# A fifth PSUM bank per pair, and one of two down tiles issued inside it

## The chip, the cores and the metric

The kernel runs on one core of a Trainium2 chip. The metric is the device time of one execution in microseconds (us); smaller is better. The core's engines are called here as the profile calls them: PE is the matmul engine TensorE and PEld its weight loads, DVE is VectorE, ACT is ScalarE, POOL is GpSimd, and SP is the engine whose queue issues nearly all loads. PSUM is the memory that matmuls write, in eight banks; only DVE and ACT read it here.

## The reference: what is computed

Two layers of a hybrid decoder, for a prompt of 512 tokens and 8 x 4 sample tokens, 544 columns in all. Model width is 1024, FFN width 2752, embedding width 256. One layer is

```
h += 0.5 * SwiGLU_a(RMSNorm(h))           # FFN, weights w1_a, w3_a, w2_a
u  = RMSNorm(h); proj = u @ w_in          # state-space heads and window attention
h += concat(ssd_out, attn_out) @ w_out
h += 0.5 * SwiGLU_b(RMSNorm(h))           # FFN, weights w1_b, w3_b, w2_b
h += sigmoid(RMSNorm(h) @ w_ple_gate) * (p[i] @ w_ple_proj)   # embedding
SwiGLU(x) = (silu(x @ w1) * (x @ w3)) @ w2
```

The outputs are h and the states and caches of both layers. There are four FFNs in the whole, and the change touches these and the last line, the embedding step.

## The kernel before

**Layout.** h is held transposed in SBUF: 8 chunks of 128 rows by 544 columns, the columns in two halves of 272. Every product is made of fp32 split into a high and a low part, three matmuls for one: weight-high x x-high, weight-high x x-low, weight-low x x-high. ACT casts the high part of a weight (L100), DVE subtracts for the low part (L101). In the profile the weights of plain products are named wh and wl, those of sums of weights qh and ql; the operands are XH and XL (norm output), T (sums of blocks of it), U (the FFN's inner activation), EH and EL (the embedding).

**FFN.** `ffn` makes 21.5 column tiles of width 128. The first tile and the rest are done plainly (`plain`). The other 20 are done by `pair`, one tile of w1 and the same tile of w3 together: a scheme of seven block products instead of eight, each 12 matmuls of 272 columns (L354). In the code's order they are f11, g2, g3, g1, f12, f22 and g4. They go to four banks: f11 and then f12 accumulate in pa, g2 in pb, g3 and then f22 in pc, g1 and then g4 in pd. Between the two uses of a bank its first content is read: ACT copies pa to v[0] (L362), DVE subtracts pb (L364), makes v[1] = v[0] - pc (L366) and c2's second half = v[1] + pd (L368). Then come c2's first half and t (L370, L372, L374), POOL's multiplication by the norm (L375), tanh on ACT (L248), DVE (L249), POOL (L250), the product c2 (L377), and the split of the result into U, high part on ACT (L259) and low part on DVE (L260). The weights' sums are made by POOL (L338, L339) and DVE (L340, L345).

**Down projection.** Every four pairs fill one U. While the next four pairs run, the eight output tiles of the U before are made, two per pair: `down` is a `gemm` of 2 x 24 / 2 matmuls, 24 per tile, into two banks (L126), and DVE adds the banks to h (L325). For the first four pairs of an FFN it is `plain_down`, of 10 matmuls per tile, with the U of `plain`. After the last pair, eight `down` tiles of the last U remain.

**Embedding.** `ple_prep` loads the embedding rows (L1115, L1116; the tile pt takes memory that the FFN held), transposes them on PE (L1122, L1124), and splits them into EH and EL (ACT L1125, L1126; DVE L1127, L1128). `ple` then runs, for each of eight output tiles, the gate product (48 matmuls with XH and XL) and the projection (12 with EH and EL). In the first tile the norm's sums (L169) and its spreading (L181) stand between them.

**What sets the order.** Each engine runs its instructions in order. That order is made when the program is built: a list scheduler takes instructions in the code's order as their priority and moves a later one ahead where it reckons an earlier one not to be ready. So the code's order is a wish, and the built order tells what runs. Banks come from one pool of eight (`bank()`).

Of the kernel before, what the change touches and what calls it, by code (L numbers as in the profile page):

```python
# [16 lines left out]
DEPTH = 2  # L17
# [6 lines left out]
HN = N // 2  # L24
# [15 lines left out]
def hymba_step(ctx: ExitStack, tc: tile.TileContext, I, O):  # L40
# [9 lines left out]
    def bank():  # L50
        return psp.tile([128, 512], F32, tag="ps", name="ps")
# [84 lines left out]
    HALF = (slice(0, HN), slice(HN, N))  # L136
# [97 lines left out]
    def ffn(g, w1, w3, w2, begun=None):  # L234
# [5 lines left out]
        with tc.tile_pool(name="ffn", bufs=2, reuse_waits="tile") as fp:  # L240
# [17 lines left out]
            def keep(U, i, u):  # L258
                A.copy(U[:, 0, i, :], u)  # L259
                V.tensor_sub(U[:, 1, i, :], u, U[:, 0, i, :].bitcast(F32))  # L260
# [64 lines left out]
                    V.scalar_tensor_tensor(h[:, m, HALF[a]], ps[a][:, 0:HN], f, h[:, m, HALF[a]], op0=ALU.mult, op1=ALU.add)  # L325


            def pair(j, sums, U, i):
                def unit(w, k, pool, tag, bufs):
                    src = w[k * 512:(k + 1) * 512, j * 128:(j + 1) * 128].rearrange("(k p) m -> p k m", p=128)  # L330
                    return raw_unit([(lambda t: t, src)], pool, tag, bufs)

                a11 = unit(w1, 0, fp, "ra", 4)
                a21, a22 = unit(w3, 0, wp, "raw", None), unit(w3, 1, wp, "raw", None)
                a12 = unit(w1, 1, fp, "ra", 4)
                f11 = split(a11)
                q1 = fp.tile([128, KU, 128], F32, tag="q1", name="q1")
                G.tensor_tensor(q1, a21, a22, op=ALU.add)  # L338
                G.tensor_tensor(a21, a21, a11, op=ALU.add)  # L339
                V.tensor_tensor(a11, a11, q1, op=ALU.add)  # L340
                g2 = split(a11, KU, fp, "q", 4)
                g3 = split(a21, KU, fp, "q", 4)
                g1 = split(q1, KU, fp, "q", 4)
                f12 = split(a12)
                V.tensor_tensor(a12, a12, a11, op=ALU.add)  # L345
                f22 = split(a22)
                g4 = split(a12, KU, fp, "q", 4)
                t2, t3, t1, t4 = sums
                x11, x21, x22 = ((XH[:, k:k + KU, c:c + HN], XL[:, k:k + KU, c:c + HN]) for k, c in ((0, 0), (KU, 0), (KU, HN)))

                def prod(ps, f, x, start):
                    for k in range(KU):
                        for n, (lhsT, rhs) in enumerate(terms3([f], k, x[0][:, k, :], x[1][:, k, :])):
                            PE.matmul(ps[:, 0:HN], lhsT, rhs, start=start and k == 0 and n == 0, stop=k == KU - 1 and n == 2,  # L354
                                      skip_group_check=not start)

                pa, pb, pc, pd = bank(), bank(), bank(), bank()
                v = fp.tile([128, 2, HN], F32, tag="v", name="v")
                t = fp.tile([128, N], F32, tag="t1", name="t")
                c2 = fp.tile([128, N], F32, tag="c2", name="c2")  # L360
                prod(pa, f11, x11, True)
                A.copy(v[:, 0, :], pa[:, 0:HN])  # L362
                prod(pb, g2, t2, True)
                V.tensor_sub(v[:, 0, :], v[:, 0, :], pb[:, 0:HN])  # L364
                prod(pc, g3, t3, True)
                V.tensor_sub(v[:, 1, :], v[:, 0, :], pc[:, 0:HN])  # L366
                prod(pd, g1, t1, True)
                V.tensor_tensor(c2[:, HALF[1]], v[:, 1, :], pd[:, 0:HN], op=ALU.add)  # L368
                prod(pa, f12, x21, False)
                V.tensor_tensor(t[:, HALF[0]], pa[:, 0:HN], Rb[:, HALF[0]], op=ALU.mult)  # L370
                prod(pc, f22, t4, False)
                V.tensor_sub(c2[:, HALF[0]], v[:, 0, :], pc[:, 0:HN])  # L372
                prod(pd, g4, x22, False)
                V.tensor_tensor(t[:, HALF[1]], v[:, 0, :], pd[:, 0:HN], op=ALU.add)  # L374
                G.tensor_tensor(t[:, HALF[1]], t[:, HALF[1]], Rb[:, HALF[1]], op=ALU.mult)  # L375
                th = gated(t)
                V.tensor_tensor(c2, c2, th, op=ALU.mult)  # L377
                keep(U, i, c2)

            def down(j0, U, m):  # L380
                src = w2[j0 * 128:(j0 + PH) * 128, m * 128:(m + 1) * 128].rearrange("(k p) m -> p k m", p=128)
# [5 lines left out]
            for j0 in range(1, NJ, PH):  # L387
                U = uset()
                for i in range(PH):
                    pair(j0 + i, sums, U, i)  # L390
                    for m in range(2 * i, 2 * i + 2):
                        last(m)
                last = lambda m, U=U, j0=j0: down(j0, U, m)
            for m in range(KD):
                last(m)
# [732 lines left out]
            V.tensor_tensor(EL[:, c, NP:N], p1[:, 0:NS], EH[:, c, NP:N].bitcast(F32), op=ALU.subtract)  # L1128
        return EH, EL

    def ple(l, P, lp, E, last):
        EH, EL = E
        wg, wpj = I["w_ple_gate"][l], I["w_ple_proj"][l]
        first = piece(wg, 0, 0, KD)
        norm = Norm(P["gp"])
# [14 lines left out]
        for m in range(KD):  # L1150
            pg = xgemm(first if m == 0 else piece(wg, 0, m * 128, KD))
            if m == 0:
                norm.sums()
            p = piece(wpj, 0, m * 128, 2)
            pe = gemm([[t for k in range(2) for t in terms3(p, k, EH[:, k, :], EL[:, k, :])]])
            if m == 0:
# [43 lines left out]
    for l in range(DEPTH):  # L1200
# [7 lines left out]
        mix(l, P)  # L1208
        ffn(P["g2"], I["w1_b"][l], I["w3_b"][l], I["w2_b"][l])
        with tc.tile_pool(name="ple", bufs=2, reuse_waits="tile") as lp:  # L1210
            E = ple_prep(l, lp)
            Pn = params(l + 1) if l + 1 < DEPTH else None
            ple(l, P, lp, E, l == DEPTH - 1)
        P = Pn


# [62 lines left out]
```

## Time and profile before

| | |
|---|---|
| median of 3 runs | 2238.54 us (2235.72 to 2247.51) |
| profiled execution | 2239.0 us, its span 2237.2 us |
| PE busy | 2132.8 us (95%), mean granted clock 0.979 |
| DVE, ACT, POOL busy | 1814.2 (81%), 963.4 (43%), 693.4 (31%) us |
| HBM read, written | 187.56 MB, 9.53 MB |
| L354, matmuls of `pair` | 6720 |

PE is the engine that is busy nearly always, so time is to be had where it stands still or where its granted clock is low. Idle time of another engine costs nothing by itself. An average over the span hides that the stages differ; the prediction reads single stages. A row of the timeline or of a group names line, engine, operation, out<-in, shapes and count; a bracket at its end gives the idle time of the engine before it and what ended it.

### The profile page before, as it was taken

The page shows a single profiled execution, that of the slowest core. Times are in us where ns is not written, and L with a number is a line of the kernel's source. Part 1 is how long each engine was busy: PE and PEld are TensorE (multiplying, and loading weights), DVE is VectorE, ACT ScalarE, POOL GpSimd, SP SyncE. Part 2 cuts the span into 40 slices and gives each one's busy share as a digit, 9 for nine tenths or more (in the row PEclk, how much of TensorE's full clock was granted, in tenths as well). Part 3 has the DMA queues.
Part 4 walks back from the last instruction along what each step waited for, and adds up shares of the span by engine and source line. Part 5 has one row for each costly group of instructions (what it writes and reads, how often), then busy time and mean ns, then how long its engine had stood idle before and what let it go on. Part 6 is the DMA issues. An engine that isn't in the chain of part 4 may idle for free.

```text
span 2237.2 us, 43389 instructions
## 1 busy us (share of the span) xinstructions
PE 2132.8 (95%) x16706; PEld 2085.6 (93%) x16706; DVE 1814.2 (81%) x3282; ACT 963.4 (43%) x1784; POOL 693.4 (31%) x601
## 2 busy tenths in 40 slices
PE   7889999999999899999988999999999998999999
PEld 6889999998899899999988999999888988999998
DVE  7898987589868899886487889975997798998854
ACT  6344443444345344444363444443443543444443
POOL 5232331233523332322132333222334333322220
PEclk9899999999999999999999999999998999999999
DMA  5343332313242333322223333333232423333222
GB/s 142 95 119 96 90 105 73 82 50 86 58 133 59 104 90 99 96 83 84 76 67 104 91 104 90 93 78 76 58 82 67 115 75 105 91 101 97 77 70 76
DMA packets 401211, 197.89 MB, mean 88 GB/s; under 512 B 40270, under 2 KB 400358, under 8 KB 401004
## 3 DMA queue, kind: packets, MB, share of 16 engines
q1 hardware_dynamic: 399420, 194.93, 31.9%
q8 instruction: 132, 2.16, 0.4%
q14 instruction: 75, 0.61, 0.1%
q10 hardware_dynamic: 1584, 0.18, 0.0%
HBM read 187.56 MB, written 9.53 MB: 88 GB/s over the span
## 4 chain that ended last, share of the span: by engine, by line
PE 68%; DVE 19%; issue 4%; POOL 4%; DMA 3%; ACT 1%; POOLq 0%; SPq 0%; DVEq 0%; ACTq 0%
PE ps L126 34%; PE ps L354 29%; DVE wl L101 4%; DVE CV L654 2%; DVE ql L101 2%; POOL th L250 1%; DMA raw<-in_w_a 1%; PE ps L900 1%; DMA raw<-in_w_b 1%; DVE wk L517 1%; DVE XL L155 1%; DVE c L377 1%; DVE ra L345 1%; POOL q L338 1%; DVE th L249 1%
## 5 line engine op out<-in xcount | busy, mean ns | idle before, releaser
L126 PE MATMUL ps<-U,wh 128*128 128x272 f32 x2752 | 526.4, 289 | 0.0
L100 ACT CAST wh<-raw 128x512 fp32r<-128x512 f32 (+1 forms) x448 | 264.8, 596 | 439.6 <-PE ps L126 241.1
L126 PEld LDWEIGHTS ps<-U,wh 128*128 128x128 f32 x2752 | 434.9, 189 | 0.0
L126 PE MATMUL ps<-U,wl 128*128 128x272 f32 x1408 | 402.3, 288 | 0.0
L101 DVE TENSOR_TENSOR wl<-raw,wh 128x512 fp32r<-128x512 f32 (+1 forms) x448 | 313.1, 702 | 72.6 <-ACT wh L100 64.9
L126 PE MATMUL ps<-XH,wh 128*128 128x272 f32 x1184 | 352.2, 300 | 8.9 <-DVE wk L517 4.3
L126 PE MATMUL ps<-XL,wh 128*128 128x272 f32 x1184 | 345.6, 293 | 4.1 <-DVE XL L155 4.0
L126 PE MATMUL ps<-XH,wl 128*128 128x272 f32 x1152 | 336.6, 293 | 0.0
L126 PEld LDWEIGHTS ps<-U,wl 128*128 128x128 f32 x1408 | 266.1, 189 | 0.0
L354 PE MATMUL ps<-T,qh 128*128 128x272 f32 x1280 | 246.7, 289 | 0.8 <-ACT qh L100 0.8
L126 PEld LDWEIGHTS ps<-XH,wh 128*128 128x128 f32 x1184 | 227.5, 193 | 14.6 <-DVE wk L517 4.7
L126 PEld LDWEIGHTS ps<-XL,wh 128*128 128x128 f32 x1184 | 228.7, 193 | 6.2 <-DVE XL L155 5.6
L338 POOL TENSOR_TENSOR q<-raw 128x512 f32<-128x512 f32 x80 | 115.3, 1442 | 353.8 <-DMA raw<-in_w_b 173.5
L126 PEld LDWEIGHTS ps<-XH,wl 128*128 128x128 f32 x1152 | 222.1, 193 | 0.0
L375 POOL TENSOR_TENSOR t<-t,Rb 128x272 f32<-128x272 f32 x80 | 68.1, 851 | 465.3 <-DVE t L374 413.4
L354 PEld LDWEIGHTS ps<-T,qh 128*128 128x128 f32 x1280 | 202.3, 189 | 1.2 <-ACT qh L100 1.2
L354 PE MATMUL ps<-XH,wh 128*128 128x272 f32 x640 | 186.0, 291 | 10.4 <-ACT v L362 7.7
L354 PE MATMUL ps<-XH,qh 128*128 128x272 f32 x640 | 187.6, 293 | 7.8 <-DVE c L368 7.8
L354 PE MATMUL ps<-T,ql 128*128 128x272 f32 x640 | 186.3, 292 | 7.5 <-DVE ql L101 7.5
L354 PE MATMUL ps<-XH,ql 128*128 128x272 f32 x640 | 188.2, 294 | 4.1 <-DVE ql L101 4.1
L101 DVE TENSOR_TENSOR ql<-ra,qh 128x512 fp32r<-128x512 f32 x160 | 183.4, 1146 | 7.7 <-ACT qh L100 0.4
L354 PE MATMUL ps<-XL,qh 128*128 128x272 f32 x640 | 188.3, 294 | 0.0
(389 smaller groups left out, 5072.8 us busy)
## 6 DMA issues: line engine op xcount, KB each, us to landing
raw<-in_w_a SPq DMA_DIRECT2D x168, 256.0 KB
raw<-in_w_b SPq DMA_DIRECT2D x168, 256.0 KB
ra<-in_w_a SPq DMA_DIRECT2D x80, 256.0 KB
ra<-in_w_b SPq DMA_DIRECT2D x80, 256.0 KB
raw<-in_w_in SPq DMA_DIRECT2D x60, 256.0 KB
raw<-in_w_ple_gate SPq DMA_DIRECT2D x32, 256.0 KB
raw<-in_w_in SPq DMA_DIRECT2D x32, 128.0 KB
raw<-in_w_out SPq DMA_DIRECT2D x32, 128.0 KB
```

The source lines that it names most:

```text
L100: A.copy(wh[:, 0:n, :], raw[:, 0:n, :])
L101: V.tensor_sub(wl[:, 0:n, :], raw[:, 0:n, :], wh[:, 0:n, :].bitcast(F32))
L126: PE.matmul(ps[a][:, 0:HN], lhsT, rhs[:, a * HN:(a + 1) * HN], start=gi == 0 and i == 0, stop=gi == n - 1 and i == len(terms) - 1)
L155: V.scalar_tensor_tensor(XL[:, c, sl], src, g[:, c:c + 1], XH[:, c, sl].bitcast(F32), op0=ALU.mult, op1=ALU.subtract)
L249: V.scalar_tensor_tensor(th[0:np_, :], th[0:np_, :], 1.0, t1[0:np_, :], op0=ALU.add, op1=ALU.mult)
L250: G.tensor_tensor(th[0:np_, :], th[0:np_, :], Rb[0:np_, :], op=ALU.mult)
L338: G.tensor_tensor(q1, a21, a22, op=ALU.add)
L345: V.tensor_tensor(a12, a12, a11, op=ALU.add)
L354: PE.matmul(ps[:, 0:HN], lhsT, rhs, start=start and k == 0 and n == 0, stop=k == KU - 1 and n == 2, skip_group_check=not start)
L375: G.tensor_tensor(t[:, HALF[1]], t[:, HALF[1]], Rb[:, HALF[1]], op=ALU.mult)
L377: V.tensor_tensor(c2, c2, th, op=ALU.mult)
L654: V.scalar_tensor_tensor(cv, pc[:, w:w + 568], P["cw"][:, w * 8 + ch:w * 8 + ch + 1], cv, op0=ALU.mult, op1=ALU.add)
```

## The change

There are three edits. `pair` takes a fifth bank, pe: f22 opens a group of its own there, and c2's first half is v[1] - pe in place of v[0] - pc; the value is the same, since v[1] is v[0] less g3's product. `pair` also takes its two down tiles as a list `between` and calls the first of them behind L368, ahead of f12, and the second at its end. `ple_prep` is called from `ple`, behind the gate's first tile and the norm's sums. Lines behind L368 have a number one higher than before up to the embedding (L374 is now L375, L377 is L378).

```
-            def pair(j, sums, U, i):
+            def pair(j, sums, U, i, between):
...
-                pa, pb, pc, pd = bank(), bank(), bank(), bank()
+                pa, pb, pc, pd, pe = (bank() for _ in range(5))
...
                 prod(pd, g1, t1, True)
                 V.tensor_tensor(c2[:, HALF[1]], v[:, 1, :], pd[:, 0:HN], op=ALU.add)
+                between[0]()
                 prod(pa, f12, x21, False)
                 V.tensor_tensor(t[:, HALF[0]], pa[:, 0:HN], Rb[:, HALF[0]], op=ALU.mult)
-                prod(pc, f22, t4, False)
-                V.tensor_sub(c2[:, HALF[0]], v[:, 0, :], pc[:, 0:HN])
+                prod(pe, f22, t4, True)
+                V.tensor_sub(c2[:, HALF[0]], v[:, 1, :], pe[:, 0:HN])
...
                 keep(U, i, c2)
+                between[1]()
...
-                    pair(j0 + i, sums, U, i)
-                    for m in range(2 * i, 2 * i + 2):
-                        last(m)
+                    pair(j0 + i, sums, U, i, [lambda m=m, last=last: last(m) for m in range(2 * i, 2 * i + 2)])
...
-    def ple(l, P, lp, E, last):
-        EH, EL = E
+    def ple(l, P, lp, last):
...
             if m == 0:
                 norm.sums()
+                EH, EL = ple_prep(l, lp)
...
-            E = ple_prep(l, lp)
             Pn = params(l + 1) if l + 1 < DEPTH else None
-            ple(l, P, lp, E, l == DEPTH - 1)
+            ple(l, P, lp, l == DEPTH - 1)
```

**DVE in one pair of the steady part.** Before, from the split of the next weights to c2's first half (L101 is a low part of a weight, L340 and L345 are sums of weights, L364 to L372 read the products out of their banks):

```order
L101 TENSOR_TENSOR wl<-ra,wh 128x512
L345 TENSOR_TENSOR ra<-ra 128x512
L364 TENSOR_TENSOR v<-v,ps 128x272
L101 TENSOR_TENSOR ql<-ra,qh 128x512
L366 TENSOR_TENSOR v<-v,ps 128x272
L101 TENSOR_TENSOR ql<-raw,qh 128x512
L368 TENSOR_TENSOR c_3662<-v,ps 128x272
L101 TENSOR_TENSOR ql<-q_3843,qh 128x512
L370 TENSOR_TENSOR t<-ps,Rb 128x272
```

and now:

```order
L101 TENSOR_TENSOR wl<-ra,wh 128x512
L364 TENSOR_TENSOR v<-v,ps 128x272
L101 TENSOR_TENSOR ql<-ra,qh 128x512
L366 TENSOR_TENSOR v<-v,ps 128x272
L345 TENSOR_TENSOR ra<-ra 128x512
L101 TENSOR_TENSOR ql<-raw,qh 128x512
L368 TENSOR_TENSOR c_2165<-v,ps 128x272
L101 TENSOR_TENSOR ql<-q_2345,qh 128x512
L325 SCALAR_TENSOR_TENSOR h<-ps,h 128x272 x2
L101 TENSOR_TENSOR wl<-raw,wh 128x512
L371 TENSOR_TENSOR t<-ps,Rb 128x272
```

L345 has moved from ahead of L364 to behind L366, and the first down tile's two additions to h (L325) now stand behind L368. Further on, between L249 and c2, both additions of the second down tile stand where one stood before. On PE, the 48 matmuls of the two down tiles that followed g4 are now 24 between g1 and f12 and 24 behind g4.

**PE at the end of the first FFN.** Before, from the last matmuls of the old U's last tile into the first tile of the new U (with buffer numbers; ps_4697 and ps_4698 are the two banks of that tile, U_3830 is the new U):

```order
L126 MATMUL ps_4664<-U_2969,wh_4659 128x272 x2
L126 MATMUL ps_4664<-U_2969,wl_4660 128x272
L126 MATMUL ps_4697<-U_3830,wh_4693 128x272 x2
L126 MATMUL ps_4697<-U_3830,wl_4694 128x272
...
L126 MATMUL ps_4697<-U_3830,wl_4694 128x272
L126 MATMUL ps_4698<-U_3830,wh_4693 128x272 x2
```

and now (ps_4717 and ps_4718, U_3846):

```order
L126 MATMUL ps_4684<-U_2981,wl_4680 128x272
L126 MATMUL ps_4717<-U_3846,wh_4713 128x272 x2
L126 MATMUL ps_4717<-U_3846,wl_4714 128x272
...
L126 MATMUL ps_4718<-U_3846,wh_4713 128x272
L126 MATMUL ps_4717<-U_3846,wh_4713 128x272
L126 MATMUL ps_4718<-U_3846,wh_4713 128x272
L126 MATMUL ps_4718<-U_3846,wl_4714 128x272
```

The scheduler now takes one matmul of the second bank ahead of the tenth of the first, which is the first to read the last chunk of the new U. Between the last pair's g4 and that one stood 48 + 9 matmuls before, and now 24 + 9 + 1.

**PE at the embedding of the first layer.** One piece of the difference: the transposes of pt and what stands around them.

```order
+L169 MATMUL ps<-ones,acc 128x1 x4
+L169 MATMUL ps<-ones,acc 32x1
 L1122 MATMUL ps<-ident,pt 128x128 x4
 L1124 MATMUL ps<-ident,pt 128x32
 L1122 MATMUL ps<-ident,pt 128x128 x4
 L1124 MATMUL ps<-ident,pt 128x32
-L193 MATMUL ps<-ident,pi 128x32
-L126 MATMUL ps<-XH,wh 128x272
-L126 MATMUL ps<-XL,wh 128x272
-L126 MATMUL ps<-XH,wl 128x272
```

The gate's first 48 matmuls and the norm's sums now come ahead of the transposes, and the first products with EH and EL follow them directly. On SP the loads of pt keep their place in the queue.

## The prediction

> **What bounds the kernel now.** I read the page first (TensorE, PE, is busy 95% of the span, VectorE, DVE, 81%), then the windows by stage, the waits of TensorE, the timeline around its last waits, and DVE's rows in one pair. Columns of the windows are the stretch, its length, then busy time (and instructions) of each engine, the granted clock, the DMA share and rate.
>
> ```profile
> core 0: us, PE busy (x) PEld busy (x) DVE busy (x) ACT busy (x) POOL busy (x), PEclk, DMA share, GB/s
> 1901.78:2117.23 215.45, 215.45 (x1718) 215.45 (x1718) 190.51 (x312) 93.18 (x156) 64.56 (x50) 1.00 0.33 91
> ...
> 44.00:175.00 131.00, 113.38 (x826) 110.09 (x826) 118.20 (x201) 51.97 (x98) 42.83 (x30) 0.95 0.36 103
> 702.00:802.00 100.00, 89.63 (x672) 87.66 (x672) 86.48 (x152) 40.21 (x76) 34.06 (x25) 0.97 0.34 94
> 1152.00:1265.00 113.00, 96.32 (x704) 94.16 (x703) 91.63 (x165) 43.89 (x83) 37.57 (x27) 0.94 0.33 92
> 1804.00:1904.00 100.00, 88.16 (x680) 85.75 (x679) 89.90 (x154) 41.02 (x78) 34.30 (x25) 1.00 0.34 95
> ```
>
> Each FFN has two halves. In the later two thirds (first window, of the fourth FFN) TensorE is busy for every microsecond at full clock: nothing that only removes waits can win there. In the first six or seven pairs (last four windows) it stands still 10 to 18 us per FFN, 56.5 us in the four, while DVE is busy for about nine tenths. The waits say for whom (us in total, times, longest):
>
> ```profile
> PE ps L354 <- DVE v L366: 25.1, 19, 3.6
> PE ps L354 <- DVE ql L101: 11.6, 7, 2.6
> ...
> PE ps L354 <- DVE c L368: 7.8, 5, 2.0
> ...
> PE ps L1122 <- DMA pt<-in_p_prompt: 6.3, 2, 3.2
> ```
>
> The largest is the one the fifth bank removes: f22 accumulates on the bank of g3 and must wait until DVE has read it at L366. What counts is the last wait of each FFN, since after it TensorE never stops again until the tail. Those last waits are all on L366, one in each FFN (the bracket is the idle time and its releaser):
>
> ```profile
> 163.11 0.40 PE L354 MATMUL ps<-T,wh 128*128 128x272 f32 x1 [2.78 <-DVE v L366]
> ...
> 790.95 0.52 PE L354 MATMUL ps<-T,wh 128*128 128x272 f32 x2 [0.96 <-DVE v L366]
> ...
> 1245.12 0.29 PE L354 MATMUL ps<-XH,wl 128*128 128x272 f32 x1
> 1248.96 0.82 PE L354 MATMUL ps<-T,wh 128*128 128x272 f32 x2 [3.56 <-DVE v L366]
> ...
> 1892.49 0.39 PE L354 MATMUL ps<-T,wh 128*128 128x272 f32 x1 [1.03 <-DVE v L366]
> ```
>
> **Part 1, the pair.** The price of a matmul comes from the chain, where a pair's 84 run in one piece and the next pair follows 16.57 us later:
>
> ```profile
> 172.40 10.57 PE ps L354 x84
> 188.97 10.57 PE ps L354 x84
> ```
>
> 10.57 / 84 = 0.126 us; the pair has 84 + 48 = 132 of them, 16.6 us, as measured. The number of instructions stays the same: one product opens a group instead of continuing one, and c2 is built from v[1]. So the steady part gains nothing, and the work is to find how far the end of the late phase moves.
>
> In that phase DVE is behind, and TensorE's end is DVE's moment plus the matmuls that remain. Before: from L366 there remain f22, g4 and both down tiles, 12 + 12 + 48 = 72 matmuls, 9.07 us. After: f22 waits for no read; the next thing that TensorE needs of DVE is L368, because g4 accumulates on pd. Behind that remain g4 and one down tile, 36 matmuls, 4.54 us. DVE reaches L368 a little later than L366, by one ql split and L368 itself; the order shows that L345 moves from before L364 to behind L366, so the work up to L368 is otherwise the same. Their starts in a steady pair:
>
> ```profile
> 985.79 1.67 DVE L345 TENSOR_TENSOR ra<-ra 128x512 f32<-128x512 f32 x1
> ...
> 989.09 0.42 DVE L366 TENSOR_TENSOR v<-v,ps 128x272 f32<-128x272 f32 x1
> 989.44 0.68 DVE L101 TENSOR_TENSOR ql<-raw,qh 128x512 fp32r<-128x512 f32 x1
> 990.04 0.42 DVE L368 TENSOR_TENSOR c<-v,ps 128x272 f32<-128x272 f32 x1
> ```
>
> 990.04 - 989.09 = 0.95 us. Gain per FFN: 9.07 - 4.54 - 0.95 = 3.58; four FFNs: **14.3 us**. From both sides: nothing, if DVE falls back by as much; at most the waits on L366 and L368 together, 32.9 us. I take 14.3, as the four last waits are of just the kind that is removed. The pairs before them do not bind harder: between pairs DVE loses time against TensorE until the last wait.
>
> Is the steady part safe? DVE's loop there also takes 16.57 us, and these are its two waits that matter:
>
> ```profile
> 993.16 0.44 DVE L374 TENSOR_TENSOR t<-v,ps 128x272 f32<-128x272 f32 x1 [0.19 <-PE ps L354]
> ...
> 997.36 0.73 DVE L377 TENSOR_TENSOR c<-c,th 128x544 f32<-128x544 f32 x1 [1.12 <-POOL th L250]
> ```
>
> Only the 0.19 is a wait for TensorE, so DVE now needs 16.38 of 16.57 us: nearly a second bound. After, both evacuations of the second down tile stand between L249 and L378, one more than before, and fill about 0.35 us of the 1.12: 16.03 us. The loop gets looser by that much in every pair, late ones too. Against it stands pair 0 of the second and fourth FFN: its first down tile now wants the second chunk of U in the middle of the pair, before f12 is through, and the queue behind it is f12's rest, f22 and g4, for which L371 to L375 wait. Before, TensorE stood there about 2 us for L368, and U's chunk was complete at 711.2, later still:
>
> ```profile
> 710.50 0.72 DVE L311 TENSOR_TENSOR U<-ur,U 64x544 fp32r<-64x544 f32 x1
> 710.53 0.39 PE L354 MATMUL ps<-XH,qh 128*128 128x272 f32 x1 [2.02 <-DVE c L368]
> ```
>
> I price it at 0 to 2.4 us in each of the two, and the looser loop at 0 to 0.35 x 6 pairs x 4 = 8.4 us; the two are set against each other at **0**.
>
> **Part 2, the end of each FFN.** This is what the change costs. Before, 48 matmuls of the old U lie between the last pair's g4 and the first that reads the new U's last chunk; after, only 24, since half of them went into the pair. The order shows 24 + 9 + 1 = 34 matmuls ahead of it. The chunk arrives so (g4 ends as L374 starts; a matmul's record lasts 0.29 us, as in the row at 1245.12, so its last one began near 1026.0):
>
> ```profile
> 1026.30 0.44 DVE L374 TENSOR_TENSOR t<-v,ps 128x272 f32<-128x272 f32 x1 [0.25 <-PE ps L354]
> ...
> 1031.34 0.65 ACT L259 CAST U<-c 128x544 fp32r<-128x544 f32 x1 [1.49 <-DVE c L377]
> ...
> 1032.17 0.72 DVE L260 TENSOR_TENSOR U<-c,U 128x544 fp32r<-128x544 f32 x1
> ```
>
> The high part is there at 1031.99. TensorE would want it at 1026.0 + 35 x 0.1258 = 1030.4, so it stands 1.6 us. Eight matmuls later (1.0 us) it wants the low part, ready at 1032.89: covered. With 0.05 us for the release, the cost is 1.65 x 4 = **6.6 us**. Lower end 4 (one microsecond each, if other rows of the tail are taken ahead), upper end 12, if each wait also halves the clock for some microseconds. I leave that out, because the window from 1804 to 1904 kept a clock of 1.00 with waits of this size:
>
> ```profile
> PE ps L354 <- DVE c L368: 2.6, 2, 1.9
> ```
>
> Between the groups inside an FFN the same chunk is wanted 24 + 48 + 9 matmuls after g4, 10.2 us, against 6.6, or 7.3 now that L340 stands ahead of L260: covered.
>
> **Part 3, the embedding.** Before, TensorE goes from the last down tile to transposes whose data have not landed, and then runs at half pace:
>
> ```profile
> 1055.02 0.50 SPq L1115 DMA_DIRECT2D pt<-in_p_prompt  x1
> ...
> 1059.51 0.80 PE L1122 MATMUL ps<-ident,pt 128*128 128x128 f32 x4 [3.18 <-DMA pt<-in_p_prompt]
> ...
> 1056.30:1059.50 3.20, 0.02 (x1) 0.03 (x1) 2.19 (x4) 1.64 (x3) 0.32 (x1) 1.00 0.82 261
> ...
> 1064.00:1066.00 2.00, 2.00 (x11) 2.00 (x10) 0.00 (x0) 0.00 (x0) 0.00 (x0) 0.50 0.00 0
> 1068.00:1070.00 2.00, 2.00 (x18) 2.00 (x17) 0.65 (x1) 0.62 (x1) 0.00 (x0) 1.00 0.00 0
> ...
> 1060.96 0.69 DVE L1127 TENSOR_TENSOR EL<-ps,EH 128x512 fp32r<-128x512 f32 x1 [1.92 <-ACT EH L1125]
> ...
> 2160.99 0.41 PE L1122 MATMUL ps<-ident,pt 128*128 128x128 f32 x2 [3.13 <-DMA pt<-in_p_prompt]
> ```
>
> The load's place in SP's queue doesn't change; it waits for memory of the FFN, so it still lands near 1059.5. After, the 48 matmuls of the gate's first tile (6.0 us) run in that gap: its last operand XL of column 7 depends on the last down tile as in every norm, and is needed only 2.6 us in. The idle goes, 3.18 + 3.13 = 6.3 us, and with it the half pace: 11 matmuls in 2 us against 18, about 0.1 us lost on each of some 19 and 13 matmuls, 3.2 us. New: the product with EH and EL now follows its transposes at once, and waits for about one such copy into EL (0.69 us, of which I count 0.6): -1.2 us in the two layers. Sum **8.3 us**; ends 4 (if the gate tile waits for XL) and 10.
>
> The Trainium skill, page "TensorE: Matmul & The Clock Gate", section "HAM oscillation — how this bites in real kernels", puts the idle time from which the clock halves at about 3.4 us. The trace halves after 3.18 us, so the rule's figure does not hold here to the letter; by it the 3.2 us would not exist, part 3 would be 5.1 and the total 2226.
>
> **Sum.** The profiled execution took 2239.0 us (span 2237.2), the median of the three runs is 2238.54, so no correction: 2239.0 - 14.3 + 0 + 6.6 - 8.3 = **2223 us**.
>
> **Rivals.** (a) DVE paces the late phase, so a wait removed at f22 comes back at L368 in full. For it: DVE is nine tenths busy in those windows, and waits on ql and L368 stand beside those on L366. Against it: it is the matmuls behind the last wait that fall from 72 to 36. Then parts 2 and 3 alone: 2239.0 + 6.6 - 8.3 = 2237. (b) Everything on L366 and L368 goes: 2239.0 - 32.9 + 6.6 - 8.3 = 2204. Against it: ql waits of 11.6 us in the same pairs would take part of the place. (c) Slower: DVE becomes the bound of the steady pairs. The order of DVE moves against POOL's two weight sums, and the rows show what a meeting costs (mean ns behind the comma):
>
> ```profile
> L345 DVE TENSOR_TENSOR ra<-ra 128x512 f32<-128x512 f32 x1 | 1.7, 1671 | 0.0
> L340 DVE TENSOR_TENSOR ra<-ra,q 128x512 f32<-128x512 f32 x1 | 0.7, 691 | 0.0
> ...
> L339 POOL TENSOR_TENSOR raw<-raw,ra 128x512 f32<-128x512 f32 x1 | 1.6, 1622 | 0.1
> L338 POOL TENSOR_TENSOR q<-raw 128x512 f32<-128x512 f32 x1 | 1.4, 1379 | 4.7 <-DMA raw<-in_w_b 4.7
> ```
>
> L345 pays 0.98 us for the same shape. POOL's sums last 3.0 us per pair; if one more microsecond of them falls on DVE than today, the loop is 17.03, 0.46 over TensorE's 16.57, in some 13 pairs x 4: +24, and the gain of part 1 is gone: 2239.0 + 24 + 6.6 - 8.3 = 2261. It decides from 0.54 us more per pair. The Trainium skill, page "SBUF — State Buffer", section "Who interferes with whom", says that such an instruction with two SBUF inputs and a POOL read exclude each other, the later one blocked whole: the rows agree, and order alone then decides who pays. That the change doesn't do what it says is excluded: the order shows the tile inside the pair and the transposes behind the gate tile.
>
> **Chances.** Forecast 0.55, with its own range 2212 to 2233 (part 1 between 4 and 25); (a) 0.25; (b) 0.12; (c) 0.08. The range, 2208 to 2241, leaves out most of (b) and (c). Half a percent, 11 us, is about what the three runs can tell from no change (they spread over 12): faster means below 2227. That is three quarters of the forecast, (b), and a little of (a): 0.55; same 0.37; slower 0.08.
>
> **What would show it.** Right: no wait of TensorE on v L366; the last wait of an FFN on c L368; each FFN's steady part starting about 3.6 us earlier; a new wait of 1.6 us on ACT U L259 at four places; TensorE idle under 1 us at the embedding, at clock 1.00. Wrong: TensorE's waits on L368 and ql grow by what L366 loses; or gaps of TensorE in the steady pairs; or the tail's wait followed by clock 0.5.

## The result, and the profile after

| | before | after |
|---|---|---|
| median of the runs taken together (four each), us | 2242.70 (2235.72 to 2247.51) | 2266.58 (2260.79 to 2269.03) |
| profiled execution, us | 2239.0 | 2260.8 |
| its span, us | 2237.2 | 2259.0 |

The ratio is 1.0104, with a 95% interval of 1.0087 to 1.0120: the changed kernel is one per cent slower. The prediction said 2223 us, with 2241 as its upper end, and a gain; it is wrong in sign.

The page of the changed kernel shows TensorE busy for longer though its instructions are the same, and DVE and POOL busy for less:

```profile
PE 2145.4 (95%) x16706; PEld 2091.3 (93%) x16706; DVE 1753.0 (78%) x3282; ACT 940.2 (42%) x1784; POOL 686.9 (30%) x601
```

The waits of TensorE after (us in total, times, longest). L366, with 25.1 us the largest before, is down to 0.9 us; waits for U and for the weights of the down tiles have come:

```profile
PE ps L126 <- ACT U L259: 16.1, 20, 2.5
PE ps L354 <- DVE c L368: 12.7, 11, 3.1
PE ps L126 <- DVE U L260: 12.1, 16, 0.9
PE ps L126 <- DVE wl L101: 10.9, 5, 3.6
...
PE ps L126 <- DVE U L311: 8.6, 2, 4.6
```

**Where the time is.** I cut each FFN by the starts of ACT's L362, one per pair, and by DVE's last L325 (lines have other numbers in some of the kernels below). The table gives sums over the four FFNs, in us, each from one profiled execution. "Ends" holds pairs 1 to 7 and the stretch from pair 18 to the last down tile; they are taken together, since TensorE's order places a pair's first product differently in the two kernels. Each total starts with the span and ends with TensorE's last matmul.

| | pairs 8 to 17 | ends | whole FFN | outside the FFNs | total |
|---|---|---|---|---|---|
| before | 663.2 | 775.6 | 1438.8 | 794.0 | 2232.8 |
| after | 683.8 | 786.9 | 1470.7 | 783.6 | 2254.3 |
| e1, embedding alone | 663.9 | 779.2 | 1443.1 | 787.9 | 2231.0 |
| e2, fifth bank alone | 664.2 | 776.1 | 1440.3 | 799.5 | 2239.7 |
| e3, moved tile alone | 688.0 | 790.2 | 1478.2 | 800.1 | 2278.3 |
| e5, after with POOL's old order | 661.7 | 776.6 | 1438.3 | 782.5 | 2220.8 |
| e6, after without L250 | 662.7 | 766.7 | 1429.4 | 790.1 | 2219.5 |

Execution by execution the part outside the FFNs moves by 6 to 8 us, and the FFNs of e1, in which nothing is changed, took 4.3 us more than before; differences of that size say nothing. Outside the FFNs the change is -10.4: the four kernels with the embedding's edit lie at 782.5 to 790.1 there, the three without it at 794.0 to 800.1. In pairs 8 to 17, which the forecast held for unable to change, it is +20.6, or 0.51 us in each of 40 pairs, far above that noise; at the ends +11.3.

**What happens in a steady pair.** First the window of eight steady pairs of the second FFN (columns as in the prediction's windows), then DVE's waits in it, for the kernel before:

```profile
835.10:967.70 132.60, 132.60 (x1058) 132.60 (x1057) 118.83 (x193) 57.55 (x97) 41.33 (x32) 1.00 0.35 96
```

```profile
DVE c L377 <- POOL th L250: 9.0, 8, 1.1
DVE t L374 <- PE ps L354: 1.7, 8, 0.2
DVE th L249 <- ACT th L248: 1.4, 8, 0.2
```

The same two views after:

```profile
849.10:985.50 136.40, 133.92 (x1057) 132.97 (x1056) 106.84 (x193) 53.61 (x97) 40.08 (x32) 1.00 0.33 94
```

```profile
DVE c L378 <- POOL th L250: 18.4, 8, 2.4
DVE th L249 <- ACT th L248: 10.9, 8, 1.4
```

Per pair before: 14.85 us busy and 1.13 + 0.21 + 0.18 us of waits, 16.4 of 16.57. After: 13.36 busy, but 2.30 + 1.36 of waits, 17.0 of 17.05. The wait for TensorE (t on L354) is no longer there: DVE does not wait for TensorE any more, its own loop (the round of dependences that comes back to DVE with every pair) is the longer one. The loop runs through POOL, and this is one round of it in the timeline of the changed kernel:

```profile
874.99 0.43 DVE L375 TENSOR_TENSOR t<-v,ps 128x272 f32<-128x272 f32 x1
875.33 0.69 DVE L101 TENSOR_TENSOR ql<-ra,qh 128x512 fp32r<-128x512 f32 x1
877.38 0.72 DVE L249 SCALAR_TENSOR_TENSOR th<-th,t 128x544 f32<-128x544 f32 x1 [1.36 <-ACT th L248]
...
881.20 1.80 DVE L378 TENSOR_TENSOR c<-c,th 128x544 f32<-128x544 f32 x1 [2.39 <-POOL th L250]
...
875.50 1.16 POOL L376 TENSOR_TENSOR t<-t,Rb 128x272 f32<-128x272 f32 x1 [10.22 <-DVE t L375]
878.55 1.30 POOL L338 TENSOR_TENSOR q<-raw 128x512 f32<-128x512 f32 x1 [1.89 <-DMA raw<-in_w_b]
879.80 1.36 POOL L250 TENSOR_TENSOR th<-th,Rb 128x544 f32<-128x544 f32 x1
881.12 1.29 POOL L339 TENSOR_TENSOR raw<-raw,ra 128x512 f32<-128x512 f32 x1
```

Of the same round before, the prediction shows L374 and L377; between them stood

```profile
993.73 1.26 DVE L101 TENSOR_TENSOR ql<-ra,qh 128x512 fp32r<-128x512 f32 x1
...
993.67 0.77 POOL L375 TENSOR_TENSOR t<-t,Rb 128x272 f32<-128x272 f32 x1 [5.06 <-DVE t L374]
```

L249 ends at 878.10, and L250 could run. It starts at 879.80, since L338 stands ahead of it in POOL's queue: a weight sum for the pair three further on, which waits 1.89 us for its load and then takes 1.30. Over the 53 rounds of the four FFNs in which L338 stands directly ahead of L250, L250 starts 1.74 us after L249's end in the mean. The wait for the load is what puts the sum in the way: by the rows, a sum begun at 876.66, as L376 ended, would have been through at 877.96, ahead of L249's end. That is worked out, not tried. Behind L250 waits DVE's L378, and behind that everything DVE does for the next pair's weights and banks. From t to c2 (start of L375 to start of L378) it is 6.21 us; before it was 4.20 (993.16 to 997.36 in the prediction's rows). A smaller part of the 2.01 us comes from ahead of tanh: before, POOL's multiplication (L375) began just ahead of DVE's ql row and took 0.77 us, and the ql row took 1.26; now the ql row is first and takes 0.69, and the multiplication (L376) takes 1.16. So tanh ends later, and DVE, which is through with its own row sooner, waits for it: the 1.36 us at L249.

In the built order of POOL, before and after:

```
before                        after
L339 raw<-raw,ra              L339 raw<-raw,ra
L375 t<-t,Rb                  L376 t<-t,Rb
L250 th<-th,Rb                L338 q<-raw
L338 q<-raw                   L250 th<-th,Rb
```

**Where TensorE pays.** Within a group of four pairs TensorE runs on at 16.6 us a pair and DVE falls behind it. The last matmul of g4 and L375, in the first and the last of three steps, and a step later, behind a group boundary:

```profile
857.06 0.29 PE L354 MATMUL ps<-XH,ql 128*128 128x272 f32 x1
857.91 0.44 DVE L375 TENSOR_TENSOR t<-v,ps 128x272 f32<-128x272 f32 x1
...
906.94 0.29 PE L354 MATMUL ps<-XH,ql 128*128 128x272 f32 x1
909.10 0.44 DVE L375 TENSOR_TENSOR t<-v,ps 128x272 f32<-128x272 f32 x1
...
917.78 0.39 PE L126 MATMUL ps<-U,wh 128*128 128x272 f32 x1 [0.38 <-ACT U L259]
919.07 0.40 PE L126 MATMUL ps<-U,wh 128*128 128x272 f32 x1 [0.89 <-DVE U L260]
...
925.33 0.29 PE L354 MATMUL ps<-XH,ql 128*128 128x272 f32 x1
926.18 0.44 DVE L375 TENSOR_TENSOR t<-v,ps 128x272 f32<-128x272 f32 x1
```

The lag grows from 0.85 to 2.16 us in three pairs, DVE needing (909.10 - 857.91) / 3 = 17.06 us for each. Then the first down tile of the next group wants the U that this lag has made late, TensorE stands, and the lag is 0.85 again. So the list of waits names U, but U may be only the place where the lag is made up; whether it is also the cause, the experiments must tell. They set two theories against each other. Theory P: POOL's new order, L338 ahead of L250, makes the loop longer. Theory U: the moved tile wants U too early, whatever POOL does. Three rivals go with them: B, that five banks cost time by themselves; C, contention, that POOL's sums meet more of DVE's rows; E, that the embedding's edit costs time.

### The profile page after: what moved, and what is told of

It reads as the page before. It is cut to its first block, busy times and chain, and to the rows that moved or that the text cites. A ratio compares the mean times of both kernels' runs of the same rounds, so it can differ in the third digit from the quotient of the medians.

```text
span 2259.0 us, 43389 instructions
## 1 busy us (share of the span) xinstructions
PE 2145.4 (95%) x16706; PEld 2091.3 (93%) x16706; DVE 1753.0 (78%) x3282; ACT 940.2 (42%) x1784; POOL 686.9 (30%) x601
## 3 DMA queue, kind: packets, MB, share of 16 engines
q8 instruction: 132, 2.16, 0.4%
## 5 line engine op out<-in xcount | busy, mean ns | idle before, releaser
L126 PE MATMUL ps<-U,wh 128*128 128x272 f32 x2752 | 540.4, 292 | 38.0 <-ACT U L259 16.1
L126 PEld LDWEIGHTS ps<-U,wh 128*128 128x128 f32 x2752 | 438.7, 191 | 46.8 <-ACT U L259 20.5
L126 PE MATMUL ps<-U,wl 128*128 128x272 f32 x1408 | 404.9, 291 | 10.9 <-DVE wl L101 10.9
L101 DVE TENSOR_TENSOR wl<-raw,wh 128x512 fp32r<-128x512 f32 (+1 forms) x448 | 318.8, 713 | 67.6 <-ACT wh L100 60.4
L126 PE MATMUL ps<-XH,wh 128*128 128x272 f32 x1184 | 351.7, 299 | 10.3 <-DVE wk L517 4.4
L126 PE MATMUL ps<-XL,wh 128*128 128x272 f32 x1184 | 345.8, 293 | 1.9 <-DVE XL L155 1.8
L126 PE MATMUL ps<-XH,wl 128*128 128x272 f32 x1152 | 336.9, 293 | 0.0
L376 POOL TENSOR_TENSOR t<-t,Rb 128x272 f32<-128x272 f32 x80 | 86.6, 1083 | 771.7 <-DVE t L375 725.9
L126 PEld LDWEIGHTS ps<-U,wl 128*128 128x128 f32 x1408 | 268.0, 191 | 12.0 <-DVE wl L101 12.0
L354 PE MATMUL ps<-T,qh 128*128 128x272 f32 x1280 | 247.5, 290 | 1.3 <-ACT qh L100 1.3
L126 PEld LDWEIGHTS ps<-XH,wh 128*128 128x128 f32 x1184 | 227.5, 193 | 15.9 <-DVE wk L517 4.8
L378 DVE TENSOR_TENSOR c<-c,th 128x544 f32<-128x544 f32 x80 | 121.1, 1514 | 143.3 <-POOL th L250 143.3
L126 PEld LDWEIGHTS ps<-XL,wh 128*128 128x128 f32 x1184 | 228.8, 193 | 3.7 <-DVE XL L155 3.2
L126 PEld LDWEIGHTS ps<-XH,wl 128*128 128x128 f32 x1152 | 222.5, 193 | 0.0
L354 PEld LDWEIGHTS ps<-T,qh 128*128 128x128 f32 x1280 | 203.0, 190 | 2.4 <-ACT qh L100 2.4
L354 PE MATMUL ps<-XH,qh 128*128 128x272 f32 x640 | 187.8, 293 | 12.8 <-DVE c L368 12.7
L354 PE MATMUL ps<-T,ql 128*128 128x272 f32 x640 | 187.1, 293 | 5.9 <-DVE ql L101 5.9
L259 ACT CAST U<-c 128x544 fp32r<-128x544 f32 x80 | 51.8, 647 | 333.9 <-DVE c L378 333.9
L354 PE MATMUL ps<-XH,wh 128*128 128x272 f32 x640 | 187.8, 293 | 2.9 <-ACT v L362 1.6
L354 PE MATMUL ps<-XH,wl 128*128 128x272 f32 x640 | 187.6, 293 | 0.1
L354 PE MATMUL ps<-XL,qh 128*128 128x272 f32 x640 | 186.9, 292 | 0.0
```

The lines of the kernel that those rows point to most:

```text
L101: V.tensor_sub(wl[:, 0:n, :], raw[:, 0:n, :], wh[:, 0:n, :].bitcast(F32))
L126: PE.matmul(ps[a][:, 0:HN], lhsT, rhs[:, a * HN:(a + 1) * HN], start=gi == 0 and i == 0, stop=gi == n - 1 and i == len(terms) - 1)
```

## The experiments

Each was timed in five rounds beside the kernel before; ratios are to that.

**The three edits apart.** e1 takes only the embedding's edit, e2 only the fifth bank, e3 only the tile inside the pair.

```
e2  +pa, pb, pc, pd, pe = (bank() for _ in range(5))
    +prod(pe, f22, t4, True); c2 first half = v[1] - pe
e3  +between[0]()  ahead of prod(pa, f12, ...), between[1]() at the end of pair
```

> The kernel before with the third edit alone (embedding transposes behind the gate's first tile). Theory P (POOL's order): the loss of the change sits in the pair; POOL's order there is that of the kernel before (L375, L250, L338, L339), so the pair's period stays at 16.57 us and the run gains what the prediction gave to part 3, 6 to 9 us: ratio 0.996 to 0.997. Theory U (the moved tile wants U sooner) expects the same. Rival E: the embedding edit costs time, because the product with EH and EL follows its transposes at once; then the ratio is 1.002 or more.

> The kernel before with the fifth bank alone; both down tiles stay behind the pair. Theory P: POOL's order is that of before, so the period stays at 16.57 us; the waits on v L366 go, and behind the last wait on c L368 there remain 60 matmuls in place of 72 behind L366, so the gain is at most (72 - 60) x 0.126 - 0.95 = 0.6 us per FFN, 2 us: ratio 0.998 to 1.001. Rival B (banks): five banks a pair and four for its down tiles go round the eight sooner and cost time by themselves: ratio 1.005 or more, with waits of L126 or L354 on the readers of a bank.

> The kernel before with the moved down tile alone, four banks, embedding as before. Theory P: here, as in the changed kernel, POOL's order has the next pair's first weight sum L338 ahead of L250, so the steady period is near 17.07 us and the run is slower than the changed kernel by the embedding's 6 to 9 us: ratio 1.012 to 1.016. Theory U expects the same time, but at the group boundaries alone. Rival B expects no loss: ratio 0.998 to 1.002.

Measured: e1 0.9967 (0.9954 to 0.9980), e2 1.0010 (0.9998 to 1.0022), e3 1.0186 (1.0171 to 1.0201). The embedding gives what was forecast (rival E falls), the bank alone neither gives nor costs (rival B falls), and the whole loss is the moved tile's. e3 is above the range that I gave it (1.012 to 1.016): without the bank the tile costs half a per cent more than in the full change, where the change and e1 leave 1.0104 + 0.0033 = 1.0137. In e2 TensorE's waits moved from one row to another, as rival (a) of the prediction has it (L366 fell to 0.9 us):

```profile
PE ps L354 <- DVE c L368: 26.6, 17, 3.3
PE ps L354 <- DVE ql L101: 14.2, 8, 3.4
```

POOL has the new order in e3, and the old one in e1 and e2. That is what theory P rests on; but the moved tile also wants U earlier, and so theory U fits these three as well.

**POOL's order, undone in the changed kernel.** e4 holds L338 behind all that the code put on POOL before it. e5 holds it only behind the L250 of the pair three ahead, its old place; the dependence orders the queue and waits for nothing (`gates` lists the L250 instructions so far).

```
e4  +tc.keep_in_program_order(G.tensor_tensor(q1, a21, a22, op=ALU.add))
e5  +s = G.tensor_tensor(q1, a21, a22, op=ALU.add)
    +if j > 3:
    +    tc.add_manual_dep(s.ins, gates[-3].ins.name, ... NoSync ..., reason="order")
```

> The changed kernel with one line more: L338 is kept behind everything that the code put on POOL before it, so that POOL runs L376, L250, L338, L339 as it did before. Theory P: the late DVE-POOL loop of 17.07 us goes back to 16.57 or less, some 0.5 us x 13 pairs x 4 = 26 us return, and 2235 us follow: ratio 0.993 to 1.000. Theory U: the loop is not at fault, the first tile of every group waits for U, and the time stays within 5 us of the changed kernel's: ratio 1.007 or more. Rival C (contention of DVE with POOL's sums, as in the prediction's rival c): the sums meet DVE's two-input rows wherever they lie; the period stays near 17 and DVE's rows are longer in sum than before.

> The changed kernel with POOL's order of before and nothing else given up: the weight sum L338 of a pair is kept behind the L250 of the pair three ahead of it, which is where it stood before (the run before this one, e4, kept it behind the L250 of the pair just ahead and took away the three pairs of lead). Theory P: L250 no longer stands behind a sum that waits for its load, DVE's loop falls from 17.07 us to TensorE's 16.57, 13 pairs x 4 x 0.5 = 26 us return: 2230 to 2242 us, ratio 0.995 to 1.000. Theory U (the first tile of each group wants U too early, whatever POOL does): the period stays at 17 us and the ratio is 1.007 or more. Rival C (contention): the period stays near 17 us, and DVE's two-input rows are longer than in the changed kernel by what L378's wait loses.

e4 met no expectation: 2741.89 us, ratio 1.2227 (1.2209 to 1.2245). The order of the four POOL rows is the old one, but they belong to other pairs: L338 now sums for the next pair and not for the third, the lead is lost, and TensorE waits for the casts of the sums in each pair, whose period is 23.9 us:

```profile
PE ps L354 <- ACT qh L100: 345.9, 80, 10.0
```

It tells how much hangs on the lead, and nothing of the theories. e5 keeps the lead: 2232.53 us, ratio 0.9937 (0.9923 to 0.9952). The loss is gone and the kernel is faster than before, by a little more than P's range (0.995 to 1.000) allowed. The same eight pairs in its trace as window, DVE's waits and POOL's rows (L376, L378, L250 are here L381, L383, L252; L338 and L339 are L340 and L344):

```profile
838.80:971.40 132.60, 132.60 (x1058) 132.60 (x1058) 112.76 (x193) 55.03 (x97) 44.05 (x33) 1.00 0.34 96
```

```profile
DVE th L251 <- ACT th L250: 10.8, 8, 1.4
DVE c L383 <- POOL th L252: 9.0, 8, 1.1
```

```profile
867.86 1.37 POOL L252 TENSOR_TENSOR th<-th,Rb 128x544 f32<-128x544 f32 x1 [1.53 <-DVE th L251]
869.18 1.29 POOL L340 TENSOR_TENSOR q<-raw 128x512 f32<-128x512 f32 x1
```

L378's wait is 1.13 us again, as before the change, TensorE is busy for all of the window, and the pair takes 16.5 to 16.6 us. Theory U, which wanted 1.007 or more, falls: the tile stands where it stood and wants U as early. Rival C falls too, since DVE's busy time per pair is 14.10 us here and 13.36 in the slow kernel: the slow one has less contention. What the step does not separate: on DVE one L325 moved behind L378 and L260 moved ahead of L340 with POOL's order. Nor was an earlier load tried, which would leave L338 where it is and take its wait away.

**The first tile's wish for U, taken away.** e7 is the changed kernel, but in the first of every four pairs both tiles stand behind the pair, so that no group boundary wants U early. (POOL has the old order in these first pairs, the new one in the other three.)

```
+if i:
     between[0]()
...
+if not i:
+    between[0]()
 between[1]()
```

> The changed kernel, but in the first of each four pairs both down tiles stand behind the pair, as before. TensorE then wants the U of the group before 24 + 12 x 7 matmuls after its g4 at the earliest, and no wait for U is left inside the FFN, but for the tail. Theory U: the loss was there, so the time falls to that of the prediction's forecast, 2223 to 2235: ratio below 0.998. Theory P: DVE's and POOL's loop still takes about 17 us in three pairs of four (POOL has L338 ahead of L250 there, the old order in the first), and DVE's lag only shows later, as waits on L368 or on weights: ratio 1.003 to 1.009.

Measured: 1.0124 (1.0104 to 1.0143), nothing regained, and a little above what P gave it too. The periods of four pairs in the second FFN are 17.2, 17.3, 14.7 and 19.8 us, 17.25 in the mean, no shorter than the changed kernel's 17.05. The waits for U are gone from the list but for the tails' 6.1 us, and the same lag is made up at the next places where TensorE needs DVE or ACT:

```profile
PE ps L354 <- DVE c L368: 41.8, 25, 6.2
PE ps L354 <- ACT v L362: 15.9, 15, 2.4
```

**L250 off the chain.** e6 is the changed kernel with the norm's factor multiplied into c2 while tanh is still to come, so that nothing of POOL stands between L249 and L378.

```
+G.tensor_tensor(c2, c2, Rb, op=ALU.mult)
-th = gated(t)
+th = gated(t, rb=False)      # (tanh + 1) * t, without the factor
```

> The changed kernel with the last POOL step taken off the chain: the norm factor is multiplied into c2 on POOL while tanh still waits (c2 = c2 x Rb behind L373), and L250 is gone; the same work, one engine less between L249 and L378. Theory P: DVE's wait of 2.4 us at L378 goes whatever POOL's order is, the period is 16.57, and U comes 2 to 3 us earlier, so that the waits on U L259 and L260 go too: 2225 to 2238 us, ratio 0.993 to 0.999. Theory U: only the waits at the group boundaries and the tails shrink, some 1.5 us x 6 x 4 at most of the 28 us on U, and the period between the boundaries stays at 17 us: ratio 1.000 to 1.006. Rival C: no gain, POOL's instruction of the same length still meets DVE: ratio 1.008 or more.

Measured: 0.9905 (0.9889 to 0.9921), better than P expected. L378's wait is gone; DVE waits for ACT in each pair and now and then for TensorE (window, then waits):

```profile
834.80:967.40 132.60, 132.60 (x1058) 132.60 (x1057) 118.79 (x193) 54.49 (x97) 46.37 (x33) 1.00 0.35 96
```

```profile
DVE th L249 <- ACT th L248: 10.9, 8, 1.4
DVE c L374 <- PE ps L355: 0.9, 3, 0.3
```

Of the 2.30 us that the wait was long, 1.49 came back as longer DVE rows (14.85 us busy against 13.36), and the loop fits all the same. Two ways of taking L338 out of the chain, with the tile left inside the pair, both undo the loss; the moved tile is the cause by way of POOL's queue.

**What the bank and the tile are worth then.** e9 is e5 with four banks.

> As e5 (POOL's order of before in the changed kernel) but with four banks: f22 accumulates on g3's bank again. It tells what the fifth bank is worth where the tile stands inside. Theory P: in the steady pairs nothing, for the 24 matmuls of the tile now stand between g3's read L366 and f22; in the early pairs TensorE waits on v L366 again, some 10 to 15 us in all as in e3: 2238 to 2247 us, ratio 0.997 to 1.000. Rival: the moved tile alone already covers L366 and the fifth bank is worth nothing: ratio within 0.002 of e5's 0.9937.

Measured: 0.9968 (0.9952 to 0.9983), at the lower edge of P's range and outside the rival's, with 10.3 us of waits on the read of g3's bank (L366, L371 there). That is e1's 0.9967: with POOL's order restored the tile alone gains nothing, and tile and bank together gain 0.9937 against 0.9967, 0.3%, 7 us. The two intervals just touch.

**A better kernel.** e8 is the kernel before with the embedding's edit and the early factor; e10 is e6 with both plain tiles behind the first pair of each FFN; e11 is e6 without the moved tile; e12 is e8 with L345 on POOL.

```
e10 +if j > 1: between[0]() inside the pair, else at its end
e12 -V.tensor_tensor(a12, a12, a11, op=ALU.add)
    +G.tensor_tensor(a12, a12, a11, op=ALU.add)
```

> The kernel before with the embedding edit and with the norm factor multiplied into c2 early (L250 off the chain), four banks, both tiles behind the pair. Theory P: the steady part is TensorE's 16.57 us and gains nothing; the late pairs gain what DVE loses today at L377, 1.1 us in each of 6 pairs x 4, at most 26 us, of which TensorE's 56 us of idle time there show 5 to 20: with the embedding's 7 us 2215 to 2230, ratio 0.988 to 0.995. Rival C: POOL's instruction now meets other DVE rows and the gain is the embedding's alone: ratio 0.996 to 0.998.

> As e6 (norm factor multiplied in early, L250 off the chain), but in the first pair of each FFN both plain down tiles stand behind the pair. In e6 TensorE waits there 8.8 us in two FFNs for the second chunk of the plain U. Theory P: these waits go and DVE's lag takes back part of it: 2214 to 2222 us, ratio 0.986 to 0.9895. Rival: DVE paces these pairs whatever TensorE waits for; the wait shows up on L369 and the ratio stays at e6's 0.9905 within 0.0015.

> The kernel before with the embedding edit, the fifth bank and the early norm factor, both tiles behind the pair: e6 without the moved tile, e8 with a fifth bank. Theory P: with the chain shortened the moved tile neither gains nor loses in the steady part; without it the waits on U and on the down tiles' weights go and waits on L369 come: within 0.003 of e6's 0.9905 and of e8's 0.9919. If the prediction's part 1 holds (36 matmuls behind the last wait in place of 60), this run is slower than e6 by about 3 us x 4, ratio 0.995 or more.

> As e8 (kernel before, embedding edit, early norm factor), with the third weight sum L345 (a12 + a11) on POOL in place of DVE. It asks whether DVE paces the early pairs: DVE loses 0.7 to 1.7 us per pair, POOL gains 1.3. Theory P: the first seven pairs of an FFN are DVE's; 0.7 us x 7 x 4 = 20 us at most come off them, 5 to 15 likely: 2212 to 2222 us, ratio 0.984 to 0.989. Rival C (contention): POOL's third sum meets DVE's rows and stretches them by as much; ratio 0.991 or more.

Measured: e8 0.9919 (0.9900 to 0.9939), e10 0.9880 (0.9857 to 0.9903), e11 0.9897 (0.9873 to 0.9921), e12 0.9928 (0.9907 to 0.9949). e10, at 2217.48 us, has the lowest median of all and beats both kernels; but e6, e10 and e11 are not told apart by their intervals, so where the tile stands hardly matters once L250 is off the chain. (e10's ratio lies in P's range, but its interval reaches into that of the rival, so the two are not decided there.) e12 gained nothing on e8: theory P's range (0.984 to 0.989) is missed, and rival C, 0.991 or more, is what came. Most of what DVE is spared comes back: over eight steady pairs it has eight rows fewer, of 13.3 us (L345 is L346 there), and is busy for only 1.4 us less; the rows that are left take 10.7 us more in sum (rows overlap a little). Those that grew are mainly two ql rows a pair, from 0.68 us each to 1.39 and 1.34 in the mean. e8's window and its L346, then e12's window:

```profile
848.90:981.50 132.60, 132.60 (x1059) 132.60 (x1058) 119.21 (x193) 57.10 (x97) 45.51 (x32) 1.00 0.35 96
...
L346 DVE TENSOR_TENSOR ra<-ra 128x512 f32<-128x512 f32 x8 | 13.3, 1666 | 0.3
```

```profile
840.00:972.60 132.60, 132.60 (x1058) 132.60 (x1057) 117.80 (x185) 56.84 (x97) 59.11 (x40) 1.00 0.35 96
```

## Why the prediction was wrong, step by step

**"Is the steady part safe?" failed.** It is the step that turned the sign: "The loop gets looser ... 16.03 us" measured 17.06. Two things in it were wrong. It looked at what DVE has to do between L249 and L378, and took the wait of 1.12 us at L378 as a hole to be filled; but the end of that hole is set by POOL, and POOL's order was not read. There L338 had moved ahead of L250, and the wait at L378 became 2.30 us. And it did not see that L249 would come later: the wait there rose from 0.18 to 1.36 us, in e5 and e6 as well. With POOL's old order the loop is not looser than before either, 14.10 + 1.35 + 1.13 = 16.58 us of which nothing is a wait for TensorE; it just fits.

**"Between the groups ... covered" failed with it.** 10.2 us stood against 7.3. In the rows above g4's last matmul begins at 906.94, U's low part is awaited at 919.07: 12.1 us, made of 2.16 us of lag, 6.21 from t to c2 and the rest.

**Rival (c) had the right number for the wrong reason.** A loop of 17.03 and 2261 us were its example; 17.06 and 2260.8 were measured, but not because POOL's sums met more of DVE's rows: DVE's busy time fell by 1.5 us per pair. So the agreement is luck. It had a chance of 0.08; POOL's built order, which could be read beforehand, would have spoken for it.

**Part 1 (-14.3) was right on the wait that goes, and its gain is not shown.** The waits on L366 went, as said, from 25.1 us to 0.9. "The last wait on c L368" and the 3.6 us earlier start are not to be seen: the ends of the FFNs in e5 take 776.6 us against 775.6 before. What took the place of L366 the term did not hold: the moved tile's weights (L126 on wl, 10.9 us) and the U of the plain tiles, which I had priced at 0 to 2.4 us in two pairs, and which cost 4.56 and 4.09 (rows below). By the ratios of e5 to e1 parts 1 and 2 together are worth -0.3%, 7 us, where the prediction had -14.3 + 6.6 = -7.7; the difference of two intervals can't tell the terms apart, and the agreement is no proof of part 1. Two figures speak against it. In e5 TensorE's waits of over 0.1 us between the first and the ninth L362 of each FFN still add up to 48.9 us, against 56.5 before, though 25.1 us on L366 went. And by e11's expectation part 1 wants e11, without the moved tile, at 0.995 or more; it came out at 0.9897, no slower than e6, which has the tile.

**Part 2 (+6.6) was right.** The tail's wait on the high part of U is there in all four FFNs, 1.51 us each for the 1.6 forecast, without a loss of clock (the reason given for that is no general rule, as the last section shows). There no weight sum stands ahead of L250 any more, so its chain is the old one. The rows of the tail in the second FFN, and of the two first pairs, in the changed kernel:

```profile
719.17 0.39 PE L126 MATMUL ps<-U,wh 128*128 128x272 f32 x1 [4.56 <-DVE U L311]
...
1049.26 0.52 PE L126 MATMUL ps<-U,wh 128*128 128x272 f32 x2 [1.51 <-ACT U L259]
...
1827.92 0.39 PE L126 MATMUL ps<-U,wh 128*128 128x272 f32 x1 [4.09 <-DVE U L311]
```

**Part 3 (-8.3) was right.** The idle time and the half pace are gone, and the new wait on EL (1.2 us) did not come. The stretch of the transposes in both layers:

```profile
1074.00:1088.00 14.00, 13.98 (x109) 13.15 (x109) 7.05 (x17) 4.66 (x12) 1.66 (x2) 1.00 0.24 70
...
2187.00:2201.00 14.00, 13.98 (x109) 13.15 (x108) 6.29 (x16) 4.55 (x11) 1.56 (x1) 1.00 0.18 50
```

From the start of DVE's last L325 to the next FFN's first L362 in the first layer, and to TensorE's last matmul in the second, the changed kernel takes 6.3 and 5.1 us less than the one before, 11 in all; e1's ratio says 7.4 us, with 4.5 to 10.3 as its interval. One term was too large by its own rows: 11 matmuls in 2 us against 18 are 0.07 us lost on each, not 0.1, and on 32 of them 2.3 us in place of 3.2.

**The sum** of the parts, without the failed step, was 16 us; e5, which differs from the change by one ordering, is 13.8 us faster than its kernel before. That it comes so near is in part luck: in the table, 11.5 of e5's 12.0 us lie outside the FFNs, where 8.3 were forecast, and 0.5 inside, where 7.7 were, though a single execution can't tell these to better than some 6 us.

## What to carry to other kernels

When a scheduler builds the order, read the new order of every engine that stands in a loop, the least busy one above all: POOL, busy for 30% of the span, set the period here by two instructions that changed places. A wait that shows up at a new place can be where a lag is made up and not its cause; take the wait away there, and if the time stays, the cause is elsewhere. And an instruction that waits for a load should not stand ahead of one on the recurring chain; taking that step off the chain (e6, 0.9905) gave more than the old order of the queue (e5, 0.9937).

## What the runs showed of the hardware

**A DVE row and a POOL row that meet run one behind the other, and the order of issue decides who pays.** L378 takes 0.73 us before, and 1.80 in the changed kernel, where it starts at 881.20, just behind POOL's L339 (881.12 to 882.41): 1.21 us until that ends, and then about 0.6 of its own. The rows ahead of tanh show both directions: the ql row takes 1.26 us where POOL's multiplication began first, and the multiplication 1.16 in place of 0.77 where the ql row began first. That is what the Trainium skill, page "SBUF — State Buffer", section "Who interferes with whom", says of a DVE instruction with two SBUF inputs. e12 adds the consequence: of 13.3 us of rows moved from DVE to POOL, 10.7 us came back as longer DVE rows.

**The length of a wait alone does not tell whether the clock halves.** The changed kernel and e5 both have a wait of 3.06 us at the same place, for the low part of a down tile's weights in the first FFN. Behind it the granted clock is 0.50 in the changed kernel and 1.00 in e5. The row and the window behind it, first of the changed kernel, then of e5:

```profile
126.00 0.60 PE L126 MATMUL ps<-U,wl 128*128 128x272 f32 x1 [3.06 <-DVE wl L101]
...
126.00:128.00 2.00, 2.00 (x9) 2.00 (x10) 1.49 (x3) 0.00 (x0) 0.00 (x0) 0.50 0.38 95
```

```profile
127.01 0.39 PE L126 MATMUL ps<-U,wl 128*128 128x272 f32 x1 [3.06 <-DVE wl L101]
...
127.00:130.00 3.00, 2.99 (x23) 2.99 (x24) 2.93 (x6) 0.26 (x1) 0.00 (x0) 1.00 0.49 126
```

Shorter waits lost it too. In the kernel before, the clock is at 0.50 shortly behind a wait of 1.88 us; in the changed kernel it stays at 1.00 behind one of 1.96 us. Kernel before, then the changed kernel:

```profile
72.03 0.39 PE L354 MATMUL ps<-XH,ql 128*128 128x272 f32 x1 [1.88 <-DVE ql L101]
...
73.70:76.00 2.30, 2.30 (x12) 2.30 (x12) 2.29 (x7) 1.55 (x3) 0.00 (x0) 0.50 0.15 43
```

```profile
751.59 0.40 PE L354 MATMUL ps<-XH,qh 128*128 128x272 f32 x1 [1.96 <-DVE c L368]
...
751.60:754.00 2.40, 2.40 (x19) 2.40 (x20) 2.40 (x6) 0.00 (x0) 0.00 (x0) 1.00 0.39 109
```

What else decides it, these runs do not show. The Trainium skill, page "TensorE: Matmul & The Clock Gate", section "HAM oscillation — how this bites in real kernels", has about 3.4 us; the waits of 3.06 us (changed kernel) and 1.88 us are below it and still lost the clock. The prediction's reason for counting no clock loss at the tails, that one window kept its clock with waits up to 1.9 us, was therefore no rule, though all four tails kept theirs.
